# Token halves of the seven products as even and odd tiles, merges from the last group's first half on, gate 1 applied in PSUM

## The chip, the cores and the metric

The kernel runs on one core of a Trainium2 chip. The metric is the device time of one execution in microseconds (us), the median of three runs. Its engines are TensorE (PE, matrix products, with its weight loads as PEld), VectorE (DVE), ScalarE (ACT), GpSimd (POOL) and SyncE (SP), which here issues all DMAs.

## What is computed

One decoder block for 1024 tokens of width 1024: sparse attention and a Mamba-2 mixer side by side, merged by two gates, an output projection, then a SwiGLU network. The part that matters:

```python
x = x + gt1 * ((g_attn * y_attn + g_ssm * y_ssm) @ w_o)
h = rms_norm(x, norm2_w) * (1.0 + sc2) + sh2
x = x + gt2 * ((silu(h @ w_gate) * (h @ w_up)) @ w_down)
return rms_norm(x, norm_f_w)
```

`y_ssm = o_ssm @ w_ssm_out` is summed over four groups of 512 channels; `gt1` (a row of 1024) depends on neither token nor `x`.

## The kernel before

All products keep float32 accuracy with operands split into a high part (a rounded copy, made by ScalarE) and a low part (a difference, made by VectorE or GpSimd), and three matmuls `hi*hi + hi*lo + lo*hi` (`mm3k`, lines 295 to 297). Order is written by hand in a small planner, `Flow`: each engine has a queue, every step says what it needs and an estimated cost, and the steps are emitted in the order in which their engine could take them by these estimates. `first=True` puts a step at the head of its queue. TensorE is fed by generators ("streams") that yield one product at a time; the first stream whose next product is ready goes. On the chip each engine runs its list strictly in that order, waiting on semaphores.

*State-space projection* (`outputs`, `ssm_job`). For group g, token half h (512 tokens) and eight blocks of 128 features ft, one product of 12 matmuls writes PSUM; VectorE adds it into `yacc` (line 1309). The last one, (3, 1), is left to `last_ssm` in the tail.

*Merge* (`merge`, line 1509). For half h and feature block ft: two DMAs bring the gate and the gated attention part, VectorE does two instructions (1519, 1520), ScalarE the high part M0 (1523), VectorE (even ft, 1527) or GpSimd (odd ft, 1525) the low part M1. The merges of half 0 are queued when the tail begins, those of half 1 follow the products of `last_ssm`, one each.

*Out-projection* (`out_proj`). `w_o` comes in column blocks of 256 (`load_wo`, n = 0 to 5, where 4 and 5 are blocks 0 and 1 once more): DMA, GpSimd multiplies with gate 1 (1498), ScalarE and VectorE split (1501, 1502). A product (n, t) takes column block n mod 4 and token tile t (128 tokens) into PSUM [128, 256], three buffers; VectorE adds it to x (1567). `order` lists the 32 products: tiles 0 to 3 with all blocks, then tiles 4 to 7. When a tile has its four blocks, `norm2` stores it, squares it (ScalarE, 1580), takes the root (VectorE, 12 small instructions, lines 259 to 269) and scales it (ScalarE, 1584); `turn_x` turns it round on TensorE (h2T, 1603) and applies scale and shift (1609, 1612).

*Seven products* (`gate_up`). The SwiGLU products are done by Strassen's scheme in the form with seven products: the moving matrix is cut into B11, B21 (first token half; features 0 to 511 and 512 to 1023) and B12, B22 (second half), and combinations T1, T2, T3, T4 of a first-half tile with a second-half tile are made by `add` and `copy` in `turn_x` (1639, 1642) as soon as the second-half tile is turned: five ScalarE steps, of VectorE t1, t2 and two low parts, of GpSimd t3, T3's and T1's low parts and t4; `split_t4` splits T4 at the end. First-half tiles are only split (1625, 1626). The results lie where M0 and M1 had the merged tile, and in E0. `gate_up` begins with the four products that need B11 and B21 alone, then B22, T2 and the others; each waits for all four tiles of its operand. The weight combinations (`ff_pieces`) share VectorE, GpSimd and ScalarE with this.

*Down projection* (`down`). For each token half, 22 steps of eight products; at step 6 of each half one DMA reads that half of x1 back (1932); `final` ends each tile.

Workspace rows of 512 columns come from a ring of 18 (`row`): two in `sl`, which first holds gate 1's row (`gt`) and is given free when wo's last block is multiplied, and sixteen in `ex`.

Of the kernel before, what the change touches and what calls it, by code (L numbers as in the profile page):

```python
# [12 lines left out]
AF = mybir.ActivationFunctionType  # L13
# [226 lines left out]
class Kern:  # L240
# [997 lines left out]
    def outputs(self):  # L1238
# [37 lines left out]
        for g in range(4):  # L1276
            for h in range(2):
                for b in range(2):
                    if (g, h) == (3, 1):
                        self.Wlast = W[3, 0], W[3, 1]  # L1280
                        return
                    w = W[g, b]
                    for m in range(4):
                        op = yield from self.ssm_job(g, h, b, m, w)
                    if h == 1:
                        w.until(op)
                        if g < 3:
                            W[g + 1, b] = self.load_ssm(g + 1, b)
            self.yT[g].until(op)
# [5 lines left out]
    def ssm_job(self, g, h, b, m, w):  # L1295
        nc = self.nc
        A, V, G, D = self.ops()
        while len(self.yTop[g]) < 4 * h + 4:
            yield None
        ft, c, s = 4 * b + m, slice(m * 128, (m + 1) * 128), slice(h * 512, (h + 1) * 512)  # L1300
        ps, yT = self.buf("mm", [128, 512], "sps"), self.yT[g]
        needs = self.yTop[g][4 * h:4 * h + 4]
        for k in range(4):
            op = yield ([w.ops[k], ps] + needs, 0.685, lambda k=k: self.mm3k(
                ps.t, k, 4, w.hi[:, k, c], w.lo[:, k, c], yT[:, 0, k, s], yT[:, 1, k, s]))
        if g == 0:
            x = A(0.48, [op, self.yacc], lambda: nc.scalar.activation(self.yacc[:, ft, s], ps.t, AF.Copy))
        else:
            x = V(0.6, [op], lambda: nc.vector.tensor_tensor(self.yacc[:, ft, s], self.yacc[:, ft, s], ps.t, op=OP.add),
                  first=(g, h) == (3, 1))  # L1310
        ps.until(x)
        self.ssmop = x
        return op
# [100 lines left out]
    def tail(self):  # L1414
# [23 lines left out]
        self.gtop = D(1.46, self.gst[2], lambda: nc.sync.dma_start(self.gt(), self.gtd[0]))  # L1438
        self.wo, self.gtuse = {}, []
        self.kept, self.t4s = [], []  # L1440
        self.norms, self.blk = [], {n: [] for n in ("B11", "B21", "T1", "B22", "T2", "T3", "T4")}
        self.acts = [[None] * 2 for _ in range(NFF)]
        for n in range(2):
            self.load_wo(n)
        for ft in range(8):
            self.merge(0, ft, [])
        for n in range(2, 4):
            self.load_wo(n)
# [35 lines left out]
    def load_wo(self, n):  # L1484

        nc, b = self.nc, n % 4
        A, V, G, D = self.ops()
        if n == 4:
            self.wo[n] = W = Weights(*(Halves(self.buf("x1t", [128, 4, 256], f"x{r}{k}_o{n}", FR) for k in range(2)) for r in range(2)))
        else:  # L1490
            self.wo[n] = W = Weights(*(self.buf(tg, [128, 8, 256], f"{tg}_o{n}", FR) for tg in ("whi", "wlo")))
        room = lambda w, k0: w.bufs[k0 // 4] if n == 4 else w
        cs = slice(256 * b, 256 * b + 256)
        for k0 in (0, 4):
            raw, ks = self.buf("raw", [128, 4, 256], f"wo{n}{k0}"), slice(k0, k0 + 4)
            d = D(1.46, [raw], lambda raw=raw, k0=k0: nc.sync.dma_start(
                raw.t, self.a["w_o"][128 * k0:128 * k0 + 512, cs].rearrange("(k p) c -> p k c", p=128)))
            d = G(2.3, [d, self.gtop], lambda raw=raw: nc.gpsimd.tensor_tensor(
                raw.t, raw.t, self.gt()[:, None, cs].to_broadcast([128, 4, 256]), op=OP.mult))
            self.gtuse.append(d)  # L1500
            x = A(0.95, [d, room(W.hi, k0)], lambda raw=raw, ks=ks: nc.scalar.activation(W.hi[:, ks], raw.t, AF.Copy))
            x = V(1.14, [x, room(W.lo, k0)], lambda raw=raw, ks=ks: nc.vector.tensor_tensor(W.lo[:, ks], raw.t, W.hi[:, ks], op=OP.subtract))
            raw.until(x)
            W.ops += [x] * 4
        if n == 5:
            for i in range(2):
                self.rings["sl"][i] = self.gtuse

    def merge(self, h, ft, needs):
# [11 lines left out]
        u.until(e)  # L1521
        m = lambda t: t[:, 2 * h + ft // 4, ft % 4]
        e = A(0.52, [e, self.M0], lambda: nc.scalar.activation(m(self.M0), y(), AF.Copy))
        if ft % 2:
            e = G(1.23, [e, self.M1], lambda: nc.gpsimd.tensor_tensor(m(self.M1), y(), m(self.M0), op=OP.subtract))
        else:
            e = V(0.6, [e, self.M1], lambda: nc.vector.tensor_tensor(m(self.M1), y(), m(self.M0), op=OP.subtract))
        self.mop[h][ft] = e

    def last_ssm(self):  # L1530

        for ft in range(8):
            op = yield from self.ssm_job(3, 1, ft // 4, ft % 4, self.Wlast[ft // 4])
            if ft % 4 == 3:
                self.Wlast[ft // 4].until(op)
            self.merge(1, ft, [self.ssmop])
        self.yT[3].until(op)
        self.yacc.until(*self.mop[0], *self.mop[1])

    def out_proj(self):  # L1540
# [5 lines left out]
        two = lambda b, t: [(b, t), (b, t + 1), (b + 1, t), (b + 1, t + 1), (b, t + 2), (b + 1, t + 2), (b, t + 3), (b + 1, t + 3)]  # L1546
        order = one(0) + two(2, 0) + [(2, t) for t in fours(4)] + [(n, t) for t in fours(4) for n in (3, 4, 5)]
        left = [4, 4, 8, 8, 4, 4]
        while self.mrg < 16:
            yield None  # L1550
        xop = [D(1.46, [self.x1[t]], lambda t=t: nc.sync.dma_start(self.x1[t].t, a["x"][t * 128:(t + 1) * 128])) for t in range(NT)]
        for n, t in order:
# [5 lines left out]
            for k in range(8):  # L1558
                m = lambda r, k=k: r[:, 2 * (t // 4) + k // 4, k % 4, 128 * (t % 4):128 * (t % 4) + 128]
# [10 lines left out]
            self.x1op[t][b] = e  # L1570
            if None not in self.x1op[t]:
                self.norm2(t, op)

    def norm2(self, t, read):
# [13 lines left out]
    def turn_x(self):  # L1588
# [3 lines left out]
        for _ in range(NT):  # L1592
            while not self.norms:
                yield None
            t, need, read = self.norms.pop(0)
            js = slice(128 * (t % 4), 128 * (t % 4) + 128)
            tfs, es = [], []
# [23 lines left out]
            f4 = lambda h, tfs=tfs: tfs[h].t.rearrange("p (k c) -> p k c", c=128)  # L1621
            if t < 4:
                for h in range(2):
# [3 lines left out]
                    self.blk[("B11", "B21")[h]].append(y)  # L1627
                self.kept.append((tfs, es))
# [294 lines left out]
    def down(self):  # L1923
# [4 lines left out]
        gn = self.buf("h32", [128, 2, 1024], "gn")  # L1928
        x2op = {}

        def load_x2(h):
            x2op[h] = D(4.3, [x2], lambda: nc.sync.dma_start(
                x2[:, 4 * h:4 * h + 4], self.x1d[4 * h:4 * h + 4].rearrange("t p c -> p t c")))

# [5 lines left out]
        for h in range(2):  # L1940
# [7 lines left out]
            for f, t, c in jobs:  # L1948
                if (f, t, c) == (6, 0, 0):
                    load_x2(h)  # L1950
                if (h, f) not in self.dl:
# [18 lines left out]
                e = V(0.6, [e, x2op[h]], lambda y=y, tt=tt, cs=cs: nc.vector.tensor_tensor(  # L1970
                    x2[:, tt, cs], x2[:, tt, cs], y.t, op=OP.add))
# [16 lines left out]
    def final(self, t, nf, nfop):  # L1988
# [362 lines left out]
```

## Time and profile before

| | us |
|---|---|
| median of three runs (2584.51 to 2589.9) | 2586.04 |
| the profiled execution | 2588.99 |
| its span, first to last instruction | 2587.2 |
| TensorE busy | 2480.7 |
| VectorE busy | 1706.9 |
| ScalarE busy | 1221.9 |
| GpSimd busy | 1021.3 |
| mean granted TensorE clock | 0.983 |

Times of the rows count from the span's start. The clock column is the share of full speed that the chip granted. A name like `ops<-whi_o,M` says which tile an instruction writes and which it reads: `sps` a state-space product, `ops` an out-projection product, `h2T` a turned tile, `gu` one of the seven products, `dps` a down product, `ex` and `sl` workspace rows, `x1r`, `whi_pc` and `wlo_pc` pieces of weights.

### The profile page before, as it was taken

The page shows a single profiled execution, that of the slowest core. Times are in us where ns is not written, and L with a number is a line of the kernel's source. Part 1 is how long each engine was busy: PE and PEld are TensorE (multiplying, and loading weights), DVE is VectorE, ACT ScalarE, POOL GpSimd, SP SyncE. Part 2 cuts the span into 40 slices and gives each one's busy share as a digit, 9 for nine tenths or more (in the row PEclk, how much of TensorE's full clock was granted, in tenths as well). Part 3 has the DMA queues.
Part 4 walks back from the last instruction along what each step waited for, and adds up shares of the span by engine and source line. Part 5 has one row for each costly group of instructions (what it writes and reads, how often), then busy time and mean ns, then how long its engine had stood idle before and what let it go on. Part 6 is the DMA issues. An engine that isn't in the chain of part 4 may idle for free. (4 is left out here: it accounts for less than half of the span.)

```text
span 2587.2 us, 39156 instructions
## 1 busy us (share of the span) xinstructions
PE 2480.7 (96%) x13806; PEld 2119.4 (82%) x13806; DVE 1706.9 (66%) x3856; ACT 1221.9 (47%) x2614; POOL 1021.3 (39%) x803
## 2 busy tenths in 40 slices
PE   5999999999999999999998999999989999999997
PEld 5999779799889898888876777788968888888886
DVE  7644887866776678664478686759776545553555
ACT  4421767666556666555556356412543223223332
POOL 2111463636263636264444232115365445442222
PEclk8999999999999999999999999999989999999999
DMA  7433322213133323222456675336222322326362
GB/s 245 133 117 120 107 83 72 77 47 107 45 90 128 105 70 92 60 88 84 127 172 225 214 228 183 106 127 203 91 68 73 95 73 75 98 87 222 119 228 78
DMA packets 226260, 308.02 MB, mean 119 GB/s; under 512 B 17416, under 2 KB 151304, under 8 KB 225552
## 3 DMA queue, kind: packets, MB, share of 16 engines
q1 hardware_dynamic: 226064, 305.52, 37.1%
q8 instruction: 109, 1.79, 0.3%
q14 instruction: 87, 0.71, 0.1%
HBM read 229.83 MB, written 75.63 MB: 118 GB/s over the span
## 5 line engine op out<-in xcount | busy, mean ns | idle before, releaser
L2107 POOL TENSOR_SCALAR P<-P,sm,gate 128x640 f32<-128x640 f32 (+7 forms) x256 | 215.4, 852 | 378.2 <-DVE sm L2104 300.0
L2178 DVE TENSOR_TENSOR kv<-tp,kv 128x512 fp32r<-128x512 f32 (+1 forms) x296 | 189.6, 657 | 118.3 <-ACT kv L2177 116.9
L2177 ACT ACTIVATE kv<-tp 128x512 fp32r<-128x512 f32 (+1 forms) x296 | 165.1, 573 | 193.2 <-PE tp L2174 187.2
L2098 ACT ACTIVATE P<-P,sm 128x640 f32<-128x640 f32 (+7 forms) x256 | 186.8, 732 | 45.2 <-DVE sm L2094 43.8
L1068 PE MATMUL o<-kv 128*128 128x512 f32 x528 | 190.7, 412 | 14.9 <-DVE kv L2178 13.4
L2089 PE MATMUL S<-kv,Q 128*128 128x384 f32 (+5 forms) x768 | 183.0, 336 | 4.2 <-DVE sm L2094 4.2
L2094 DVE CUSTOM_DVE_ANT_0 P<-S,kb 128x256 f32<-128x256 f32 (+5 forms) x256 | 120.5, 495 | 62.7 <-PE tp L2174 33.9
L295 PE MATMUL fps<-hT_hi,whi_x 128*128 128x512 f32 x384 | 157.8, 411 | 0.0
L2174 PE MATMUL tp<-id,P 128*128 128x128 f32 x1056 | 154.9, 274 | 0.0
L1116 DVE SCALAR_TENSOR_TENSOR u<-xr,hcw,u 128x512 f32<-128x512 f32 x144 | 142.2, 988 | 17.6 <-ACT u L1119 12.8
L295 PE MATMUL fps<-whi_z,hT_hi 128*128 128x256 f32 x512 | 151.5, 296 | 0.1
L297 PE MATMUL fps<-hT_hi,wlo_x 128*128 128x512 f32 x384 | 150.9, 393 | 0.0
L296 PE MATMUL fps<-hT_lo,whi_x 128*128 128x512 f32 x384 | 150.6, 392 | 0.0
L2174 PEld LDWEIGHTS tp<-id,P 128*128 128x128 f32 x1056 | 128.7, 141 | 21.5 <-issue 0.4
L2089 PEld LDWEIGHTS S<-kv,Q 128*128 128x128 f32 x768 | 129.4, 190 | 20.6 <-DVE sm L2094 6.2
L297 PE MATMUL fps<-whi_z,hT_lo 128*128 128x256 f32 x512 | 145.8, 285 | 0.0
L296 PE MATMUL fps<-wlo_z,hT_hi 128*128 128x256 f32 x512 | 145.7, 284 | 0.0
L1068 PEld LDWEIGHTS o<-kv 128*128 128x128 f32 x528 | 96.4, 191 | 34.7 <-DVE kv L2178 19.0
L1826 DVE TENSOR_TENSOR ex<-ex,gu 128x512 f32<-128x512 f32 x103 | 69.6, 683 | 74.0 <-PE gu L297 55.4
L295 PE MATMUL gu<-M,x1r 128*128 128x512 f32 x292 | 116.5, 399 | 1.9 <-ACT M L1642 1.9
L296 PE MATMUL gu<-M,x1r 128*128 128x512 f32 x292 | 116.8, 400 | 0.4 <-DVE M L1639 0.4
L297 PE MATMUL gu<-M,x1r 128*128 128x512 f32 x292 | 116.3, 398 | 0.0
(434 smaller groups left out, 7767.9 us busy)
## 6 DMA issues: line engine op xcount, KB each, us to landing
wd<-w_down SPq DMA_DIRECT2D x44, 512.0 KB, 3.4
wada<-w_ada SPq DMA_DIRECT2D x40, 512.0 KB, 4.5
ac<-acd SPq DMA_DIRECT2D x32, 512.0 KB, 4.2
raw_x<-w_in SPq DMA_DIRECT2D x24, 512.0 KB, 4.5
ff<-w_gate SPq DMA_DIRECT2D x22, 512.0 KB
ff<-w_up SPq DMA_DIRECT2D x22, 512.0 KB, 5.3
actd<-ex SPq DMA_DIRECT2D x39, 256.0 KB, 3.1
ex<-actd SPq DMA_DIRECT2D x38, 256.0 KB, 3.7
```

Source lines behind the costliest of these rows:

```text
L295: mm(ps, lh, rh, start=k == 0, stop=False)
L296: mm(ps, lh, rl, start=False, stop=False)
L297: mm(ps, ll, rh, start=False, stop=k == kt - 1)
L1068: nc.tensor.matmul(o.t.rearrange("p h q -> p (h q)"), vst(), pair()[m], start=n + m == 0, stop=n == u.total - 1 and m == 1)
L1116: nc.vector.scalar_tensor_tensor(u.t, xr[:, k:k + N2], hcw[:, ft, k:k + 1], u.t, op0=OP.mult, op1=OP.add)
L2089: mm(sp[:, :w], q, kvb.kv[:, br, r, first + c0:first + c1], start=r == 0, stop=r == 1)
L2094: nc.vector.tensor_tensor_reduce(P[:, c0:c1], sp[:, :w], k.kb[:, m0:m0 + w], scale=-1.0, scalar=sm[:, 0, h:h + 1] if p else 3.0e38, op0=OP ...
L2098: ex = A(0.26 + 0.8333e-3 * n, [mx], lambda: nc.scalar.activation(P[:, :n], P[:, :n], AF.Exp, bias=sm[:, 1, h:h + 1], scale=-1.0, accum_ou ...
L2107: nc.gpsimd.tensor_scalar(P[:, :n], P[:, :n], sm[:, 3, m:m + 1], k.gate[:, i, self.h0 + m, br + 1:br + 2], op0=OP.mult, op1=OP.mult)
L2174: nc.tensor.transpose(tp[:, h * 128:h * 128 + 128], P, k.id)
L2177: hi = A(0.064 + 0.104 * n, [op, pair], lambda: nc.scalar.activation(pair()[0][:, c], tp[:, c], AF.Copy))
L2178: lo = V(0.068 + 0.133 * n, [hi], lambda: nc.vector.tensor_sub(pair()[1][:, c], tp[:, c], pair()[0][:, c]))
```

## The change

Three things. First, the state-space products of (3, 0) are moved into `last_ssm` too, in the same order as before; each is followed by its merge, and `yacc`'s accumulation is put first in VectorE's queue for the whole last group. All four first blocks of `w_o` are queued at the beginning of the tail. Second, the halves of the seven products are the even and the odd tiles: `merge` writes M0 and M1 by parity, `order` takes tiles 4 and 6 before 5 and 7 for the last three blocks, an odd tile t is combined with t-1, and the down projection's halves are even and odd tiles, for which both halves of x1 are read back at step 6 of the first half. Third, `w_o` is no longer multiplied by gate 1; a VectorE instruction multiplies each product in PSUM, before the sum. The second low part of wo block 4 goes to GpSimd. `sl` keeps gate 1 until the last such instruction.

```diff
@@ outputs
-                    if (g, h) == (3, 1):
+                    if (g, h) == (3, 0):
@@ ssm_job
-                  first=(g, h) == (3, 1))
+                  first=g == 3)
@@ tail
-        for n in range(2):
-            self.load_wo(n)
-        for ft in range(8):
-            self.merge(0, ft, [])
-        for n in range(2, 4):
+        for n in range(4):
             self.load_wo(n)
@@ load_wo
-            d = G(2.3, [d, self.gtop], lambda raw=raw: nc.gpsimd.tensor_tensor(
-                raw.t, raw.t, self.gt()[:, None, cs].to_broadcast([128, 4, 256]), op=OP.mult))
-            self.gtuse.append(d)
...
-            x = V(1.14, [x, room(W.lo, k0)], lambda raw=raw, ks=ks: nc.vector.tensor_tensor(W.lo[:, ks], raw.t, W.hi[:, ks], op=OP.subtract))
+            E, eng, cost = (G, nc.gpsimd, 2.3) if n == 4 and k0 else (V, nc.vector, 1.14)
+            x = E(cost, [x, room(W.lo, k0)], lambda raw=raw, ks=ks, eng=eng: eng.tensor_tensor(
+                W.lo[:, ks], raw.t, W.hi[:, ks], op=OP.subtract), first=n > 3)
@@ merge
-        m = lambda t: t[:, 2 * h + ft // 4, ft % 4]
+        m = lambda r: r.t.rearrange("p (t b) k (j c) -> p t b k j c", t=2, c=128)[:, :, ft // 4, ft % 4, 2 * h:2 * h + 2]
+        y4 = lambda: y().rearrange("p (j t c) -> p t j c", t=2, c=128)
...
@@ last_ssm
-        for ft in range(8):
-            op = yield from self.ssm_job(3, 1, ft // 4, ft % 4, self.Wlast[ft // 4])
-            if ft % 4 == 3:
-                self.Wlast[ft // 4].until(op)
-            self.merge(1, ft, [self.ssmop])
+        for h in range(2):
+            for ft in range(8):
+                op = yield from self.ssm_job(3, h, ft // 4, ft % 4, self.Wlast[ft // 4])
+                if h and ft % 4 == 3:
+                    self.Wlast[ft // 4].until(op)
+                self.merge(h, ft, [self.ssmop])
@@ out_proj
-        order = one(0) + two(2, 0) + [(2, t) for t in fours(4)] + [(n, t) for t in fours(4) for n in (3, 4, 5)]
+        order = one(0) + two(2, 0) + [(2, t) for t in fours(4)] + [(n, t) for n in (3, 4, 5) for t in (4, 6)] + [(n, t) for t in (5, 7) for n in (3, 4, 5)]
...
-            e = V(0.34, [op, xop[t]], lambda ps=ps, t=t, cs=cs: nc.vector.tensor_tensor(
+            e = V(0.34, [op, self.gtop], lambda ps=ps, cs=cs: nc.vector.tensor_tensor(
+                ps.t, ps.t, self.gt()[:, cs], op=OP.mult), first=True)
+            e = V(0.34, [e, xop[t]], lambda ps=ps, t=t, cs=cs: nc.vector.tensor_tensor(
                 self.x1[t][:, cs], self.x1[t][:, cs], ps.t, op=OP.add), first=True)
@@ turn_x
-            if t < 4:
+            if t % 2 == 0:
...
-            (r11, r21), old = self.kept[t - 4]
+            (r11, r21), old = self.kept[t - 1]
...
-            old = old + self.blk["B11"] + self.blk["B21"]
+            old = old + self.done2[t - 1]
@@ down
-                if (f, t, c) == (6, 0, 0):
-                    load_x2(h)
+                if (h, f, t, c) == (0, 6, 0, 0):
+                    for u in range(2):
+                        x2op.append(D(4.3, [x2], lambda u=u: nc.sync.dma_start(
+                            x2[:, 4 * u:4 * u + 4], self.x1d[4 * u:4 * u + 4].rearrange("t p c -> p t c"))))
...
-                tt, cs, y = 4 * h + t, slice(512 * c, 512 * c + 512), self.row()
+                tt, cs, y = 2 * t + h, slice(512 * c, 512 * c + 512), self.row()
@@ final
-            if t < 4:
+            if t % 2 == 0:
```

## Rows read from the trace of the kernel before

**Rows 1.** The page, part 1: busy time, share and instructions of TensorE.

```profile
PE 2480.7 (96%) x13806; PEld 2119.4 (82%) x13806; DVE 1706.9 (66%) x3856; ACT 1221.9 (47%) x2614; POOL 1021.3 (39%) x803
```

**Rows 2.** Stretches: length, then PE, PEld, DVE, ACT, POOL busy, clock, DMA share, GB/s.

```profile
1725.00:1747.00 22.00, 22.00 (x99) 18.22 (x98) 8.30 (x13) 2.25 (x4) 4.78 (x2) 1.00 0.56 207
1747.00:1768.00 21.00, 21.00 (x94) 17.38 (x93) 19.93 (x29) 5.69 (x8) 5.60 (x4) 1.00 0.65 200
1768.00:1878.20 110.20, 101.62 (x818) 99.74 (x817) 91.97 (x166) 51.93 (x88) 52.41 (x26) 0.97 0.41 134
1878.20:1918.00 39.80, 28.78 (x104) 21.63 (x104) 34.71 (x48) 19.85 (x37) 27.43 (x19) 0.83 0.23 73
1918.00:2571.00 653.00, 653.00 (x2815) 528.35 (x2814) 337.05 (x447) 203.64 (x361) 261.25 (x192) 1.00 0.34 113
```

**Rows 3.** TensorE's waits, 1768 to 1792: waiting line, releaser, sum, times, longest.

```profile
PE ops L297 <- POOL M L1525: 1.9, 1, 1.9
PE ops L297 <- DVE M L1527: 1.6, 1, 1.6
PE ops L295 <- DVE x L1567: 1.2, 2, 1.0
```

**Rows 4.** TensorE's waits, 1792 to 1878.2.

```profile
PE h2T L1603 <- ACT x L1584: 3.4, 4, 1.4
PE ops L296 <- DVE wlo_o L1502: 0.5, 1, 0.5
```

**Rows 5.** TensorE's waits, 1878.2 to 1918.

```profile
PE h2T L1603 <- ACT x L1584: 3.4, 1, 3.4
PE gu L296 <- DVE E L1639: 2.3, 1, 2.3
PE gu L295 <- ACT M L1642: 1.9, 1, 1.9
PE gu L295 <- ACT whi_pc L1692: 1.5, 1, 1.5
PE gu L297 <- DVE wlo_pc L1694: 1.5, 1, 1.5
PE gu L296 <- DVE M L1639: 0.4, 1, 0.4
```

**Rows 6.** Groups, GpSimd then VectorE, 1718 to 1918: busy, mean ns, idle before, releasers.

```profile
L1498 POOL TENSOR_TENSOR wo<-wo,sl 128x1024 f32<-128x1024 f32 x12 | 32.2, 2701 | 94.2 <-DMA wo<-w_o 79.0 <-DVE wlo_o L1502 11.8 <-DVE x L1567 3.4
...
L1639 POOL TENSOR_TENSOR M<-ex,M 128x512 fp32r<-128x512 f32 x4 | 7.0, 1740 | 0.0
...
L1520 DVE TENSOR_TENSOR yacc<-mg 128x512 f32<-128x512 f32 x16 | 17.2, 1096 | 0.0
...
L1519 DVE SCALAR_TENSOR_TENSOR mg<-mg,yacc 128x512 f32<-128x512 f32 x16 | 13.1, 846 | 0.0
L1309 DVE TENSOR_TENSOR yacc<-yacc,sps 128x512 f32<-128x512 f32 x19 | 13.0, 686 | 20.3 <-PE sps L297 20.1
...
L1527 DVE TENSOR_TENSOR M<-yacc,M 128x512 fp32r<-128x512 f32 x8 | 8.2, 1027 | 0.1
```

**Rows 7.** Timeline of VectorE and ScalarE: start us, duration us, instruction.

```profile
1784.28 2.87 DVE L1520 TENSOR_TENSOR yacc<-mg 128x512 f32<-128x512 f32 x1
1787.07 0.41 DVE L1567 TENSOR_TENSOR x<-x,ops 128x256 f32<-128x256 f32 x1
...
1882.57 0.42 DVE L1567 TENSOR_TENSOR x<-x,ops 128x256 f32<-128x256 f32 x1
...
1894.11 1.15 ACT L1584 ACTIVATE x<-x,rq_n 128x1024 f32<-128x1024 f32 x1 [2.24 <-DVE rq_n L264]
...
1905.54 1.76 DVE L1639 TENSOR_TENSOR E<-ex,E 128x512 fp32r<-128x512 f32 x1
```

**Rows 8.** Line 1567: its instructions, ns min/median/max, first and last start.

```profile
L1567 DVE TENSOR_TENSOR x<-x,ops x32: 406/412/423, 1783.1 to 1882.6; 128x256 f32<-128x256 f32 x32
```

**Rows 9.** Line 1932: its two loads of half of x1 each, issue to landing.

```profile
DMA to landing us min/median/max: 9.4/9.4/9.4
```

More of the change, by code (lines that the diff above doesn't have):

```diff
@@ L1438, in tail @@
         self.gtop = D(1.46, self.gst[2], lambda: nc.sync.dma_start(self.gt(), self.gtd[0]))
-        self.wo, self.gtuse = {}, []
-        self.kept, self.t4s = [], []
+        self.wo = {}
+        self.done2 = {}
+        self.kept, self.t4s = {}, []
         self.norms, self.blk = [], {n: [] for n in ("B11", "B21", "T1", "B22", "T2", "T3", "T4")}
         self.acts = [[None] * 2 for _ in range(NFF)]
-        for n in range(2):
-            self.load_wo(n)
-        for ft in range(8):
-            self.merge(0, ft, [])
-        for n in range(2, 4):
+        for n in range(4):
             self.load_wo(n)
@@ L1497, in load_wo @@
                 raw.t, self.a["w_o"][128 * k0:128 * k0 + 512, cs].rearrange("(k p) c -> p k c", p=128)))
-            d = G(2.3, [d, self.gtop], lambda raw=raw: nc.gpsimd.tensor_tensor(
-                raw.t, raw.t, self.gt()[:, None, cs].to_broadcast([128, 4, 256]), op=OP.mult))
-            self.gtuse.append(d)
             x = A(0.95, [d, room(W.hi, k0)], lambda raw=raw, ks=ks: nc.scalar.activation(W.hi[:, ks], raw.t, AF.Copy))
-            x = V(1.14, [x, room(W.lo, k0)], lambda raw=raw, ks=ks: nc.vector.tensor_tensor(W.lo[:, ks], raw.t, W.hi[:, ks], op=OP.subtract))
+            E, eng, cost = (G, nc.gpsimd, 2.3) if n == 4 and k0 else (V, nc.vector, 1.14)
+            x = E(cost, [x, room(W.lo, k0)], lambda raw=raw, ks=ks, eng=eng: eng.tensor_tensor(
+                W.lo[:, ks], raw.t, W.hi[:, ks], op=OP.subtract), first=n > 3)
             raw.until(x)
             W.ops += [x] * 4
-        if n == 5:
-            for i in range(2):
-                self.rings["sl"][i] = self.gtuse
     def merge(self, h, ft, needs):
@@ L1521, in merge @@
         u.until(e)
-        m = lambda t: t[:, 2 * h + ft // 4, ft % 4]
-        e = A(0.52, [e, self.M0], lambda: nc.scalar.activation(m(self.M0), y(), AF.Copy))
+        m = lambda r: r.t.rearrange("p (t b) k (j c) -> p t b k j c", t=2, c=128)[:, :, ft // 4, ft % 4, 2 * h:2 * h + 2]
+        y4 = lambda: y().rearrange("p (j t c) -> p t j c", t=2, c=128)
+        e = A(0.52, [e, self.M0], lambda: nc.scalar.activation(m(self.M0), y4(), AF.Copy))
         if ft % 2:
-            e = G(1.23, [e, self.M1], lambda: nc.gpsimd.tensor_tensor(m(self.M1), y(), m(self.M0), op=OP.subtract))
+            e = G(1.23, [e, self.M1], lambda: nc.gpsimd.tensor_tensor(m(self.M1), y4(), m(self.M0), op=OP.subtract))
         else:
-            e = V(0.6, [e, self.M1], lambda: nc.vector.tensor_tensor(m(self.M1), y(), m(self.M0), op=OP.subtract))
+            e = V(0.6, [e, self.M1], lambda: nc.vector.tensor_tensor(m(self.M1), y4(), m(self.M0), op=OP.subtract))
         self.mop[h][ft] = e
     def last_ssm(self):
-        for ft in range(8):
-            op = yield from self.ssm_job(3, 1, ft // 4, ft % 4, self.Wlast[ft // 4])
-            if ft % 4 == 3:
-                self.Wlast[ft // 4].until(op)
-            self.merge(1, ft, [self.ssmop])
+        for h in range(2):
[4 more added lines that the diff above has]
+                self.merge(h, ft, [self.ssmop])
         self.yT[3].until(op)
@@ L1546, in out_proj @@
         two = lambda b, t: [(b, t), (b, t + 1), (b + 1, t), (b + 1, t + 1), (b, t + 2), (b + 1, t + 2), (b, t + 3), (b + 1, t + 3)]
-        order = one(0) + two(2, 0) + [(2, t) for t in fours(4)] + [(n, t) for t in fours(4) for n in (3, 4, 5)]
-        left = [4, 4, 8, 8, 4, 4]
+        order = one(0) + two(2, 0) + [(2, t) for t in fours(4)] + [(n, t) for n in (3, 4, 5) for t in (4, 6)] + [(n, t) for t in (5, 7) for n in (3, 4, 5)]
+        left, gtuse = [4, 4, 8, 8, 4, 4], []
         while self.mrg < 16:
@@ L1558, in out_proj @@
             for k in range(8):
-                m = lambda r, k=k: r[:, 2 * (t // 4) + k // 4, k % 4, 128 * (t % 4):128 * (t % 4) + 128]
+                m = lambda r, k=k: r[:, 2 * (t % 2) + k // 4, k % 4, 64 * (t - t % 2):64 * (t - t % 2) + 128]
                 op = yield ([W.ops[k], self.mop[t // 4][k], ps], 0.356, lambda: self.mm3k(
@@ L1570, in out_proj @@
             self.x1op[t][b] = e
+            gtuse.append(e)
             if None not in self.x1op[t]:
                 self.norm2(t, op)
+        for i in range(2):
+            self.rings["sl"][i] = gtuse
     def norm2(self, t, read):
@@ L1595, in turn_x @@
             t, need, read = self.norms.pop(0)
-            js = slice(128 * (t % 4), 128 * (t % 4) + 128)
+            js = slice(64 * (t - t % 2), 64 * (t - t % 2) + 128)
             tfs, es = [], []
@@ L1627, in turn_x @@
                     self.blk[("B11", "B21")[h]].append(y)
-                self.kept.append((tfs, es))
+                    self.done2.setdefault(t, []).append(y)
+                self.kept[t] = tfs, es
                 continue
@@ L1928, in down @@
         gn = self.buf("h32", [128, 2, 1024], "gn")
[L1929 to L1933, printed above, removed]
+        x2op = []
         for h in range(2):
@@ L1969, in down @@
                 ps.until(e)
-                e = V(0.6, [e, x2op[h]], lambda y=y, tt=tt, cs=cs: nc.vector.tensor_tensor(
+                e = V(0.6, [e, x2op[tt // 4]], lambda y=y, tt=tt, cs=cs: nc.vector.tensor_tensor(
                     x2[:, tt, cs], x2[:, tt, cs], y.t, op=OP.add))
```

## The prediction

> **What bounds the kernel now.** I read the page first. TensorE is busy for 2480.7 us, 96% of the span [rows 1], so a change gains only where TensorE idles or runs at the lower clock. The stretches by stage come next [rows 2]. While the state-space products of the last group run (1725 to 1768), TensorE is full at clock 1.00. From 1918 to 2571 (all but the first of the seven products, and the down projection) it is full again, with no wait. Between them lie the out-projection (1768 to 1878.2, 101.62 of 110.20 us busy, clock 0.97) and the turn into the seven products (1878.2 to 1918, 28.78 of 39.80 us, clock 0.83). All that this change can give back is there.
>
> The idle time, from TensorE's waits: start of the out-projection 1.9 + 1.6 + 1.2 = 4.7 us [rows 3], rest of it 3.4 + 0.5 = 3.9 us [rows 4], the turn 3.4 + 2.3 + 1.9 + 1.5 + 1.5 + 0.4 = 11.0 us [rows 5]. Together 19.6 us, which is what the stretches leave: (110.20 - 101.62) + (39.80 - 28.78) [rows 2]. The two clock levels are 1.2 and 2.4 GHz, so a mean of 0.97 over 110.2 us costs 0.03 x 110.2 = 3.3 us of work and 0.83 over 39.8 us costs 6.8 us; part of the slow time fell on idle time, so I take 3.1 and 6.0. The clock fell behind the idle stretches only, as the full stages at 1.00 show. Loss of this region: start 7.8, middle 3.9, turn 17.0, sum 28.7 us. A change that hides everything here ends 28.7 us earlier.
>
> Who is late? VectorE. It is busy 19.93 of 21 us while the first merges run and 91.97 of 110.20 us in the out-projection, but 8.30 of 22 us in the 22 us before [rows 2]: merging starts with group 3's second half, so eight merges queue beside eight more, beside wo's low parts. GpSimd makes it worse: a 128x512 sum takes VectorE 686 ns in the mean where one operand lies in PSUM [rows 6], while one of two SBUF operands took 2.87 us beside GpSimd's gate multiplication [rows 7], and the sixteen of that kind 1096 ns in the mean [rows 6].
>
> **Part by part.**
>
> **Merges begin with (3, 0).** The eight products of (3, 0) are the same work at the same place (TensorE is full either way). What moves is the merging of half 0: eight merges of two instructions of about 0.69 us, four low parts on VectorE and four on GpSimd, from 1747 on into 1725 to 1750. The instruction after a 2.87 us one starts 0.08 us before that one's end [rows 7], so by starts a merge costs 1.2 us, a low part and an accumulation 0.6 each. The 22 us of eight products [rows 2] are 5.5 us per two, in which VectorE gets 2 x 0.6 + 2 x 1.2 + 0.6 = 4.2 us: 77%, plus what GpSimd's low part blocks. With the means of the merges as they ran beside the gate (0.846, 1.096, 1.027) [rows 6] it is 2 x 0.686 + 2 x 1.942 + 1.027 = 6.28 us, and TensorE would be held back 0.8 us per pair, 6.3 us over eight pairs. Those means come from beside GpSimd's 128x1024 instructions, which go; the remaining block is one 128x512 instruction per pair. I take 1 us (0 to 6.3). The merges' sixteen DMA pairs are spread from two bursts to one pair per 2.7 us behind the wo loads on SP; eight buffers let them run ahead, so nothing. At 1768 half 0 lies merged since some 16 us and half 1 is 2 to 5 us from it, used only 16 products later, so the first two waits of [rows 3] and the clock's fall behind them go; x's loads find their buffers earlier too. Start after: 1 us in place of 7.8.
>
> **Gate 1 in PSUM.** Removed: twelve GpSimd instructions, 32.2 us, mean 2701 ns [rows 6], each a step of 2.4 us or more between wo's load and its split, and each a block for VectorE. Added: 32 VectorE multiplications of 128x256 in PSUM. No row shows an instruction that reads and writes PSUM. The nearest is the sum that follows it, 406 to 423 ns in all 32 [rows 8], never stretched by GpSimd; by starts 0.08 us less, 0.33. I take that: 32 x 0.33 = 10.6 us of VectorE, less than the blocks that go (the merges' 16 sums, 16 products and 8 low parts ran at 1096, 846 and 1027 instead of 686 ns: 6.6 + 2.6 + 2.7 = 11.9 us). From below, nothing is gained by it; from above, 1.76 us as for a contended 128x512 [rows 7]. In the chain of a tile it adds one step of 0.4 us. The 0.5 us wait for wo's low part [rows 4] goes, since wo 5's chain loses 2.4 us and is first used two products later.
>
> The Trainium skill, "SBUF — State Buffer", section "Who interferes with whom", says that a VectorE instruction with two SBUF inputs and a GpSimd instruction that reads SBUF exclude each other for a whole instruction, and that one with at most one SBUF input doesn't take part. The trace agrees on both (2.87 us against 406 to 423 ns). By it the new multiplication is free of GpSimd, and the price 10.6 us stands; but the combinations that move ahead (next part) would bring GpSimd's blocks into the middle.
>
> **wo 4's second low part** goes from VectorE to GpSimd (at most the 2.7 us of a gate instruction of the same shape [rows 6]); its column block is first used at product 23, so free.
>
> **Even and odd halves.** A combination of tiles needs a pair (t-1, t), until now (t-4, t). Four VectorE, four GpSimd and five ScalarE instructions per pair: two of the four sets move from the end into the middle, where tiles 1 and 3 are ready after products 12 and 16 of 32; tiles 4 and 6 need only the simple split. In the turn about 2 x 7 us of GpSimd (1.74 us each [rows 6]) and 2 x 3 to 2 x 7 us of VectorE disappear. What stays is the last tile's own chain, and here I am careful. Before: the last product ends near 1878.4, its sum starts at 1882.57 behind queued work, the normalised tile leaves ScalarE at 1894.11 + 1.15 = 1895.3, its T2 low part ends at 1905.54 + 1.76 = 1907.3 [rows 7]: 29 us. Four products of 2.7 us that need only the even half (10.9 us) cover part of it, as before. After: no 4.2 us delay of the sum (1 us with the gate), the square root and the scaling 6 to 10 us instead of 12.7 since tile 5's set still runs through it, combinations 6 to 9 us: 13 to 20 us against 11 of cover, then the third products. That leaves 2 to 9 us idle, and half as much of the clock again. TensorE's order is fixed from estimates, so part of the waits for the normalised tile stays. Turn after: 8.5 us (3 to 17).
>
> Middle after: the waits for the normalised tiles (3.4 us [rows 4]) lose the gate's blocks and gain those of the combinations. I take 3.5 us (2 to 7).
>
> **Rest.** Two rows of workspace come free only at the end of the out-projection: 16 of 18 remain, and fewer tiles are held at once: nothing. x1 is read back in two loads in a row (9.4 us each to landing [rows 9]) in place of one per half; the stage has no TensorE wait with one such load in each half, and weights are loaded three steps ahead: nothing (0 to 9.4). The final steps are the same in number and order.
>
> **Sum.** After: 1 + 3.5 + 8.5 = 13.0 us of loss for 28.7 before: 15.7 us less. The profiled execution took 2588.99 us, 1.8 us around its span of 2587.2; so 2571.5 of span, 2573.3 in all. The median of the three runs is 2586.04, 2.95 below the profiled one; the same difference gives 2570.3, and I say 2570.
>
> **Rivals.**
> *All hidden.* If VectorE, freed from GpSimd, brings the last tile in 13 us, the loss is 0 + 2 + 3 = 5: 2562. For: VectorE's blocks were the cause in [rows 6]. Against: the square root still queues behind combinations.
> *The turn stays.* If the last tile's chain is as long as before (all its steps remain, the pair before it still ends 8.5 us ahead), only the start and 0.4 of the middle go: 7.2 us, 2579.
> *VectorE holds the merging stage.* TensorE full at 1725 to 1768 becomes its waiting place, 6.3 instead of 1 us: 2576.
> *Slower: the gate's multiplication is dear.* VectorE's demand in the out-projection is 92 us now; about 22 us of merges and their blocks and 12 of other blocks go, 10 of combinations come: 68 us + 32 p for the 98 us that TensorE needs. From p = 0.94 us it bounds; at p = 1.76 us the stage grows by 26 us: 2596. Against: the same PSUM operand at 406 to 423 ns.
> *It does not do what it says* is excluded: the four products that open the turn use only the even half, whose last tile is ready six products earlier.
>
> **How the numbers follow.** Forecast (10 to 21 us less) 0.47; all hidden 0.16; turn stays 0.20; merging stage 0.07; neither gain nor loss 0.04; slower 0.06. The range takes the bounds 5 us (2562) and the turn that stays with a larger middle: 2561 to 2582. 0.2% is 5.2 us, about what a measurement of this kernel can tell from no change: faster 0.47 + 0.16 + 0.15 + 0.07 = 0.85 (a quarter of the turn that stays falls within 0.2%), same 0.05 + 0.04 = 0.09, slower 0.06.
>
> **What would show it.** Right: no TensorE wait for M at the start of the out-projection and clock 1.00 there; TensorE full through the sixteen last state-space products; sums and gate at about 0.41 us; out-projection over 9 to 10 us earlier; idle of the turn under 7 us. Wrong: accumulations late with TensorE idle in the state-space products, a gate multiplication near 0.9 us, or waits for the normalised tile or T2 as long as before.

## The result, and the profile after

The changed kernel took 2564.33 us in the median of 4 runs (2557.07 to 2567.39), the kernel before 2587.97 us beside it: ratio 0.9904, 95% interval 0.9877 to 0.993. Measured again (`a_again`, below): 2566.4 us against 2585.36, ratio 0.992 (0.9904 to 0.9937), so 19 to 24 us less. The forecast was 2570 us, and its sum 15.7 us less than before.

The profiled execution took 2557.07 us, 31.9 us less than that of before. Not all of it is the change. When the k-th matmul of one trace is set beside the k-th of the other, 13.4 us of the distance are there at the first state-space product (`sps`, of group 0), ahead of everything that the change touches. The largest steps (4.3, 2.6, 1.5, 4.8 us) lie where the clock fell in the trace of before, in code that is the same; others, of up to 1.6 us, go both ways. The stretches from 60 us to that product, before and after (columns as in [rows 2]):

```profile
60.00:1541.60 1481.60, 1438.46 (x8798) 1257.79 (x8796) 1028.87 (x2693) 823.32 (x1888) 621.96 (x525) 0.99 0.36 111
60.00:1528.20 1468.20, 1431.59 (x8794) 1251.36 (x8793) 1027.97 (x2693) 822.43 (x1887) 623.70 (x525) 1.00 0.36 112
```

TensorE's work took 6.9 us longer there before, and its idle time was 6.5 us longer. In the other traces that product starts anywhere from 1532.2 to 1546.2 us, without order. I therefore compare stages, from the first matmul of one kind to the first of the next:

| stage, us | before | after | difference |
|---|---|---|---|
| all state-space products, first `sps` to first `ops` | 226.6 | 226.5 | -0.1 |
| out-projection, first `ops` to first `gu` | 110.1 | 97.9 | -12.2 |
| seven products, first `gu` to first `dps` | 447.9 | 441.8 | -6.1 |
| down projection | 245.8 | 245.7 | -0.1 |

That is 18.3 to 18.5 us less for what was changed, close to the 19.0 of the repeat. First the stretches of after, which answer to [rows 2] (length, then PE, PEld, DVE, ACT, POOL busy, clock, DMA share, GB/s):

```profile
1711.50:1733.50 22.00, 22.00 (x99) 18.22 (x98) 19.27 (x29) 5.97 (x10) 4.45 (x3) 1.00 0.83 288
1733.50:1754.50 21.00, 21.00 (x95) 17.38 (x94) 20.12 (x28) 6.32 (x9) 5.22 (x3) 1.00 0.41 135
1754.50:1852.60 98.10, 97.13 (x819) 96.68 (x818) 76.13 (x180) 48.77 (x82) 26.76 (x17) 1.00 0.43 149
1852.60:1892.40 39.80, 32.46 (x131) 24.28 (x130) 31.90 (x52) 20.93 (x37) 26.57 (x18) 0.91 0.24 73
1892.40:2539.00 646.60, 646.60 (x2788) 523.23 (x2787) 337.45 (x444) 201.74 (x358) 257.92 (x189) 1.00 0.34 114
```

VectorE now merges through both first stretches (19.27 us of 22 where it had 8.30, then 20.12 of 21), and TensorE stays full. In the out-projection TensorE works 97.13 of 98.10 us, and VectorE falls from 91.97 to 76.13 us, GpSimd from 52.41 to 26.76. The turn keeps a hole: TensorE is busy 32.46 of 39.80 us, at clock 0.91.

TensorE's waits (line, releaser, sum, times, longest). There is none from 1700 to 1778, where [rows 3] had 4.7 us. From 1778 to 1852.6, for [rows 4]:

```profile
PE h2T L1603 <- ACT x L1584: 1.0, 2, 0.5
```

and from 1852.6 to 1900, for [rows 5]:

```profile
PE gu L295 <- ACT x1r L1693: 2.9, 1, 2.9
PE gu L296 <- DVE E L1640: 2.0, 1, 2.0
PE h2T L1603 <- DVE ex L1612: 1.1, 1, 1.1
PE gu L296 <- DVE M L1640: 0.5, 1, 0.5
PE gu L295 <- DVE ex L1612: 0.5, 1, 0.5
PE h2T L1603 <- ACT ex L1609: 0.3, 1, 0.3
```

From 1900 to 2560 none again. The new instruction and the sum behind it (line 1564, was 1567), ns min/median/max, as in [rows 8]:

```profile
L1562 DVE TENSOR_TENSOR ops<-ops,sl x32: 417/432/433, 1759.8 to 1854.2; 128x256 f32<-128x256 f32 x32
...
L1564 DVE TENSOR_TENSOR x<-x,ops x32: 403/420/422, 1760.7 to 1855.2; 128x256 f32<-128x256 f32 x32
```

Groups of VectorE over 1704 to 1892.4 that answer to [rows 6] (1512 and 1513 are the merge's two instructions, 1521 its low part; busy, mean ns, idle before):

```profile
L1512 DVE SCALAR_TENSOR_TENSOR mg<-mg,yacc 128x512 f32<-128x512 f32 x16 | 13.2, 828 | 1.8 <-DMA mg<-mgd 1.6
...
L1513 DVE TENSOR_TENSOR yacc<-mg 128x512 f32<-128x512 f32 x16 | 12.5, 787 | 0.2
...
L1521 DVE TENSOR_TENSOR M<-yacc,M 128x512 fp32r<-128x512 f32 x8 | 6.0, 747 | 0.1
```

The merge's sums fell from 1096 to 787 ns and its low parts from 1027 to 747; the products hardly (846 to 828).

The timeline of the last tile and of the wait that is new, for [rows 7] (start, duration, instruction; in brackets the idle time before it and its releaser). The last `ops` matmul ends at 1852.8; the first row is the tile's last sum, the second the low part of its T2, the third a combination of weights:

```profile
1855.20 0.41 DVE L1564 TENSOR_TENSOR x<-x,ops 128x256 f32<-128x256 f32 x1
...
1872.47 1.75 DVE L1640 TENSOR_TENSOR E<-ex,E 128x512 fp32r<-128x512 f32 x1
...
1877.54 1.75 DVE L1712 TENSOR_TENSOR ex<-ff,ex 128x512 f32<-128x512 f32 x1
```
```profile
1858.95 1.15 ACT L1584 ACTIVATE x<-x,rq_n 128x1024 f32<-128x1024 f32 x1
...
1879.32 0.63 ACT L1693 ACTIVATE x1r<-ex 128x512 fp32r<-128x512 f32 x1 [2.74 <-DVE ex L1712]
```
```profile
1880.00 0.79 PE L295 MATMUL gu<-M,x1r 128*128 128x512 f32 x1 [2.90 <-ACT x1r L1693]
```

The tile's chain, from the last matmul to the end of that low part, is 1874.2 - 1852.8 = 21.4 us (29 before). The longest single wait left belongs to no token tile: VectorE makes a combination of *weights* (1712) at 1877.54, ScalarE splits it (1693), and the third product with the second weight matrix can start only then.

### The profile page after: what moved, and what is told of

It is laid out like the page before. It is cut to its first block, busy times and chain, and to the rows that moved or that the text cites. A ratio compares the mean times of both kernels' runs of the same rounds, so it can differ in the third digit from the quotient of the medians.

```text
span 2555.3 us, 39172 instructions
## 1 busy us (share of the span) xinstructions
PE 2467.0 (97%) x13806; PEld 2108.4 (83%) x13806; DVE 1698.1 (66%) x3887; ACT 1221.9 (48%) x2614; POOL 992.9 (39%) x792
## 5 line engine op out<-in xcount | busy, mean ns | idle before, releaser
L1827 DVE TENSOR_TENSOR ex<-ex,gu 128x512 f32<-128x512 f32 x117 | 79.0, 684 | 121.6 <-PE gu L297 110.0
L1068 PEld LDWEIGHTS o<-kv 128*128 128x128 f32 x528 | 95.4, 189 | 32.5 <-DVE kv L2177 16.8
L295 PE MATMUL gu<-M,x1r 128*128 128x512 f32 x296 | 117.5, 397 | 2.9 <-ACT x1r L1693 2.9
L1695 POOL TENSOR_TENSOR x1r<-wd,x1r 128x512 fp32r<-128x512 f32 x41 | 54.8, 1337 | 168.1 <-ACT x1r L1693 161.4
L296 PE MATMUL gu<-M,x1r 128*128 128x512 f32 x296 | 117.9, 398 | 0.5 <-DVE M L1640 0.5
```

Of the source, the lines that this page charges most:

```text
L295: mm(ps, lh, rh, start=k == 0, stop=False)
L296: mm(ps, lh, rl, start=False, stop=False)
L1068: nc.tensor.matmul(o.t.rearrange("p h q -> p (h q)"), vst(), pair()[m], start=n + m == 0, stop=n == u.total - 1 and m == 1)
```

## The experiments

The theory: the start was lost to merges that came too late, the middle to GpSimd's gate instructions, the turn to combinations made after the last tiles, so the three parts give their gains one by one. The rival: VectorE's in-order queue is the one cause, and the parts replace each other or depend on each other. The stages of these kernels, in us (one profiled execution of each; the rows `e1` to `e4` ran on one chip, where the kernel before took 2588.95):

| kernel | time | out-projection | seven products |
|---|---|---|---|
| before | 2588.99 | 110.1 | 447.9 |
| `e1_merges` | 2581.43 | 101.8 | 449.2 |
| `e2_gate` | 2577.24 | 102.2 | 448.5 |
| `e3_halves` | 2586.1 | 113.4 | 439.7 |
| `e4_merges_gate` | 2569.93 | 97.9 | 450.4 |
| `e10_gate_halves` | 2573.47 | 102.5 | 441.1 |
| after | 2557.07 | 97.9 | 441.8 |

**The merges alone.** The kernel before, with

```diff
-                    if (g, h) == (3, 1):
+                    if (g, h) == (3, 0):
...
+        for h in range(2):
+            for ft in range(8):
...
+                self.merge(h, ft, [self.ssmop])
```

and, as in the change, `yacc`'s accumulation first in VectorE's queue and all four blocks of `w_o` queued at the beginning of the tail.

> Kernel before with the first part alone: the products of (3, 0) and the merges that follow them in last_ssm. Measures: out-projection stage, from the first out-projection matmul to the first of the seven products (before 110.1 us, changed kernel 97.9), and seven-product stage, from there to the first down-projection matmul (447.9 and 441.8). Theory (the start was late because sixteen merges queued on VectorE in one place): out-projection 102 to 104, no wait for M at its start. Rival (it was late because GpSimd's gate multiplications block VectorE): 108 or more, the waits for M stay. Seven-product stage within 1.5 us of 447.9 by both.

The out-projection became 8.3 us shorter (101.8 us, just under the theory's 102 to 104). The stretch, columns as above, and TensorE's waits in it, 1767.2 to 1869:

```profile
1767.20:1869.00 101.80, 97.95 (x818) 96.69 (x817) 77.95 (x152) 48.50 (x82) 44.41 (x24) 1.00 0.41 144
```
```profile
PE h2T L1600 <- ACT x L1581: 3.3, 3, 1.4
PE ops L296 <- DVE wlo_o L1498: 0.4, 1, 0.4
PE ops L295 <- DVE x L1564: 0.2, 1, 0.2
```

The loss at the start is gone and the clock is 1.00, while the middle stands as in [rows 4]. In the last sixteen state-space products TensorE waits 0.6 us, once, for an accumulation into `yacc`, although GpSimd's gate instructions still ran beside the merges. The whole state-space stage took 229.7 us, 3.1 more than before; the changed kernel has it at 226.5 and 228.5 in two profiles, so I don't lay that on the merges.

**The gate alone.** The kernel before, without GpSimd's multiplication in `load_wo`, with the low parts of `w_o`'s blocks 4 and 5 placed as in the change, and with

```diff
+            e = V(0.34, [op, self.gtop], lambda ps=ps, cs=cs: nc.vector.tensor_tensor(
+                ps.t, ps.t, self.gt()[:, cs], op=OP.mult), first=True)
```

> Kernel before with the third part alone: gate 1 applied in PSUM by VectorE, wo without GpSimd's multiplication. Measures as in e1_merges. Theory (merges queue in one place): VectorE still has sixteen merges around the start, out-projection 104 to 107. Rival (GpSimd's blocks): 99 to 101, waits for M gone. Seven-product stage within 2 us of 447.9 by both.

It gave 7.9 us in the out-projection: 102.2 us, which is neither the theory's 104 to 107 nor the rival's 99 to 101. Waits there, 1764.6 to 1866.8:

```profile
PE ops L295 <- DVE x L1565: 2.5, 1, 2.5
PE ops L296 <- DVE wlo_o L1500: 0.6, 1, 0.6
```

The waits for the normalised tiles are gone, and so are both waits for M at the start: merges that are as late as before, but not blocked, come almost in time. Left at the start is a wait of 2.5 us for x, and the clock is 0.98. So the waits for M have two cures, either of which is enough. 8.3 and 7.9 don't add up to 16.2; with both it is 12.2 (`e4`).

**The halves alone.** The kernel before with the parity layout, the order of products and the two loads of x1 together.

```diff
-        order = one(0) + two(2, 0) + [(2, t) for t in fours(4)] + [(n, t) for t in fours(4) for n in (3, 4, 5)]
+        order = one(0) + two(2, 0) + [(2, t) for t in fours(4)] + [(n, t) for n in (3, 4, 5) for t in (4, 6)] + [(n, t) for t in (5, 7) for n in (3, 4, 5)]
...
-            (r11, r21), old = self.kept[t - 4]
+            (r11, r21), old = self.kept[t - 1]
```

> Kernel before with the second part alone: even and odd tiles as halves, the new order of products, both loads of x1 in the first half of the down projection; merges and gate as before. Theory (the combinations of tiles 1 and 3 moved out of the turn shorten it): seven-product stage 441 to 443. Rival (the turn is shorter because VectorE comes to it without a backlog from merges and gate): 446 or more. Out-projection 108 to 112 by both. The down projection has no TensorE wait by both.

The stretch of the out-projection and its wait for normalised tiles:

```profile
1769.50:1882.90 113.40, 102.30 (x817) 100.89 (x816) 91.47 (x168) 53.19 (x89) 55.05 (x29) 0.95 0.39 131
```
```profile
PE h2T L1605 <- ACT x L1586: 5.4, 3, 2.8
```

The turn gave 8.2 us and the out-projection took 3.3 back: the waits for normalised tiles grew from 3.4 to 5.4 us, with GpSimd at 55.05 us and clock 0.95. Beside the gate in PSUM the halves cost the out-projection 0.3 us (`e10`, below, against `e2`) or nothing (after against `e4`). So what the halves move into the middle is paid there as long as the gate runs on GpSimd.

**Merges and gate, without the halves.** `e1` and `e2` together.

> First and third part together, halves as before. Theory: out-projection 97 to 100, seven-product stage 446 to 449, so that the even and odd tiles alone give the 6 us of the turn. Rival (the turn follows VectorE's backlog): seven-product stage 443 or less.

The out-projection is that of after, 97.9 us at clock 1.00. All of the loss in the turn stays and grows by 2.5 us (450.4 us, over the theory's 446 to 449). Its waits for weights, 1857.9 to 1899, and the longest of them:

```profile
PE gu L297 <- DVE x1r L1692: 8.6, 2, 5.0
PE gu L295 <- ACT x1r L1690: 2.9, 1, 2.9
```
```profile
1866.29 0.80 PE L297 MATMUL gu<-M,x1r 128*128 128x512 f32 x1 [4.98 <-DVE x1r L1692]
```

`x1r` are pieces of weights. The wait of 2.9 us that surprised in the turn of after was already there, for the same product. The longest, 5.0 us, comes in the second of the fourteen products: the low part that it needs stands in VectorE's queue behind combinations of tile 6, which in after needs only its simple split; there this wait is gone. In all, waits for weights are 11.5 us here against 3.0 in [rows 5], and those for token tiles 2.3 against 8.0: 2.8 us more in sum, which is about what the turn grew by.

**Gate and halves, merges late.** `e2` and `e3` together.

> Gate in PSUM and even/odd halves, merges as in the kernel before. Theory (the start is on time only with both, the early merges and GpSimd without the gate): out-projection 101 to 103 as with the gate alone (102.2), seven-product stage 441 to 443 as in the changed kernel. Rival (the early merges are needless beside the other two): 99 or less.

The out-projection's waits:

```profile
PE ops L295 <- DVE x L1567: 2.8, 1, 2.8
PE h2T L1606 <- ACT x L1587: 1.0, 2, 0.5
```

Seven products 441.1, as after; out-projection 102.5 with the wait of 2.8 us for x at its start and clock 0.98. The early merges are needed for the last 4.6 us. In the out-projection the rival holds: the parts replace each other and depend on each other. In the turn the gain is the halves'. That the three single gains add up nearly to the whole in the out-projection (8.3 + 7.9 - 3.3 = 12.9 against 12.2) is chance: 12.2 comes from two of them. Merges and halves without the gate were not run.

**Is the gate's multiplication hidden?** After, with the multiplication made twice (gate 1 squared):

```diff
+            e = V(0.34, [e, self.gtop], lambda ps=ps, cs=cs: nc.vector.tensor_tensor(
+                ps.t, ps.t, self.gt()[:, cs], op=OP.mult), first=True)
```

> Changed kernel with the gate's VectorE multiplication in PSUM done twice (32 more instructions of 128x256; gate 1 enters squared). Measures: out-projection stage (97.9 us in the changed kernel, 97.9 with merges and gate alone) and seven-product stage (441.8). Theory (0.42 us by duration and 0.33 by starts, VectorE has 22 of 98 us free): out-projection 98 to 99, seven-product stage up to 1 longer, since the last tile's chain has one more step of 0.4 us. Rival (VectorE bounds the out-projection, the price of a multiplication shows in full): 106 or more.

And after without it (gate 1 left out):

```diff
-            e = V(0.34, [op, self.gtop], lambda ps=ps, cs=cs: nc.vector.tensor_tensor(
-                ps.t, ps.t, self.gt()[:, cs], op=OP.mult), first=True)
-            e = V(0.34, [e, xop[t]], lambda ps=ps, t=t, cs=cs: nc.vector.tensor_tensor(
+            e = V(0.34, [op, xop[t]], lambda ps=ps, t=t, cs=cs: nc.vector.tensor_tensor(
```

> Changed kernel without the gate's multiplication at all (gate 1 is left out of the computation), which prices the 32 instructions by their absence. Theory (the first 32 are hidden, the second 32 of e5_gate_twice were not): out-projection 97 to 98 against 97.9, seven-product stage 440 to 442 against 441.7. Rival (they cost as much as the second 32, 4.7 and 2.3 us): 93 to 95 and 439 or less; for the out-projection this can be but little, as TensorE idles 1 us there.

| | none (`e9`) | once (after) | twice (`e5`) |
|---|---|---|---|
| out-projection | 98.1 | 97.9 | 102.6 |
| VectorE busy in it | 67.85 | 76.13 | 83.10 |
| seven products | 441.2 | 441.8 | 444.0 |
| time | 2572.11 | 2557.07 | 2577.53 |

The out-projection of `e5`, and TensorE's waits in it:

```profile
1768.00:1870.60 102.60, 98.18 (x817) 97.78 (x816) 83.10 (x207) 47.94 (x82) 26.25 (x17) 0.98 0.41 143
```
```profile
PE h2T L1605 <- ACT x L1586: 2.4, 1, 2.4
PE ops L296 <- DVE x_o L1497: 2.0, 1, 2.0
```

The first 32 cost at most 0.6 us in these two stages. VectorE's busy time grows by 8.28 / 32 = 0.26 us for each; that is a net figure, since in `e9` other VectorE instructions ran longer (the splits of line 1626, 1624 there, 1013 ns in the mean against 680). (`e9`'s whole time is the longer one: its first `sps` came at 1543.9, by the chance above.) The second 32 cost 7 us, between the theory and the rival, though VectorE still had 19 us free by its busy time: TensorE waits 2.4 us for a normalised tile and 2.0 us for a low part of `w_o`, at clock 0.98. Free time in the sum was no cover here. The planner also emits another order when steps are added or left out (the longest wait in `e9`'s turn is 5.0 us for a low part of a token tile), and this and the longer chain of a tile were not told apart.

**Are GpSimd's blocks what keeps the turn long?** After, with the token combinations of GpSimd on VectorE:

```diff
-            t3 = add(G, [t1, es[1]], b12, b22, b12)
+            t3 = add(V, [t1, es[1]], b12, b22, b12)
...
-            t3l = add(G, [t3h], T3l, b12, T3h)
-            t4 = add(G, [t2], b21, b21, u2)
-            t1l = add(G, [t1h, t2], T1l, b11, T1h)
+            t3l = add(V, [t3h], T3l, b12, T3h)
+            t4 = add(V, [t2], b21, b21, u2)
+            t1l = add(V, [t1h, t2], T1l, b11, T1h)
```

> Changed kernel with the four GpSimd steps of each tile pair's combinations (t3, low parts of T1 and T3, t4) on VectorE. Theory (a GpSimd step of 1.7 us blocks VectorE for about 1.1 us, its own VectorE time is 0.6 us, so the rest of the turn's loss is GpSimd's blocks): seven-product stage 436 to 440 against 441.8. Rival (VectorE's queue is the bound and sixteen more instructions, 9.6 us, lengthen it): 443 or more. Out-projection 97 to 99 by both.

and, beyond that, T4's low parts and the first block's weight combinations on VectorE too:

> As e6_comb_dve, and the split of T4 and the GpSimd steps of the first two weight blocks on VectorE too, so that GpSimd does next to nothing from the out-projection to the thirteenth of the seven-product stage's products. Theory (blocks): 434 to 439 in the seven-product stage, VectorE's 128x512 instructions there at 0.69 us and none near 1.75. Rival (VectorE is the bound): 444 or more.

The same group of combinations in the turn, first after, then `e7_turn_dve` (busy, mean ns, idle before), and the turn of `e7_turn_dve`:

```profile
L1640 DVE TENSOR_TENSOR ex<-ex 128x512 f32<-128x512 f32 x4 | 5.1, 1291 | 0.0
```
```profile
L1640 DVE TENSOR_TENSOR ex<-ex 128x512 f32<-128x512 f32 x8 | 5.3, 686 | 0.0
```
```profile
1870.50:1912.00 41.50, 32.42 (x132) 25.23 (x131) 32.99 (x68) 21.67 (x39) 8.53 (x6) 0.88 0.23 70
```

With GpSimd at 8.53 us in place of 26.57 the blocks are gone from this group: 686 ns each, twice the work in the same time. The Trainium skill, "SBUF — State Buffer", section "Who interferes with whom", says that a VectorE instruction with two SBUF inputs contends with a GpSimd instruction that reads SBUF; the trace agrees, with 1291 and 686 ns. Yet the seven products took 442.2 (`e6`) and 443.0 (`e7`) against 441.8, not the 434 to 440 of the theory. So to move this work to VectorE gains nothing; what the blocks alone cost it doesn't tell, since VectorE has more to do (68 instructions in the turn against 52). The out-projection, which I had not expected to change, took 105.1 and 103.8 against 97.9, with waits of 3.9 and 2.9 us for a low part of `w_o`: its last one started 79 and 78 us after the stage's first matmul, and 70 us in after. What was left to test is the order in VectorE's queue.

**The same kernel again.** No edit, to see how far its time and stages vary.

> The changed kernel once more, timed in five rounds. Theory (18 us come from the out-projection and the turn; the 13 us by which its first profile was ahead at the first state-space product are chance, as that product starts between 1528 and 1542 us in six profiles of unchanged code ahead of it): ratio 0.992 to 0.994, 16 to 20 us; first state-space product again anywhere in 1528 to 1542. Rival (the changed order also shortens what lies ahead): 0.990 or less, and the first state-space product at 1528 to 1530.

2566.4 us in the median of 6 (2562.63 to 2569.8); stages 97.9 and 441.7 us. So in two profiles of this kernel these two stages repeat within 0.1 us while the whole varies by 7; the state-space stage doesn't (228.5 against 226.5). In its merging stretch TensorE waits 0.4 us once for `yacc`.

**Another order of the seven products.** If the weight combinations for the second matrix are late, products that don't need them should go first. After, with

```diff
-        seq = [(0, 0, 1), (1, 0, 1), (0, 0, 2), (1, 0, 2), (0, 0, 3), (0, 0, 6), (1, 0, 3), (0, 0, 7), (1, 0, 6), (0, 0, 5), (1, 0, 7),
+        seq = [(0, 0, 1), (1, 0, 1), (0, 0, 2), (1, 0, 2), (0, 0, 3), (0, 0, 6), (0, 0, 7), (0, 0, 5), (1, 0, 3), (1, 0, 6), (1, 0, 7),
```

(first the weight matrix, then the block, then the product).

> Changed kernel with another order of the first fourteen of the seven-product stage's products: after B22 and T2 of the first weights come their T3 and T1 and only then the second weights' B22. Theory (what is left of the turn is VectorE's queue; the second weights' combinations are the last to come through it, and the product that waits 2 to 3 us for them stands ahead of two that need none of them): the wait of gu for ACT x1r falls under 1 us, seven-product stage 437.5 to 440 against 441.7, total 2 to 4 us under the changed kernel's 2566. Rival (T3's and T1's low parts on GpSimd are as late, so the wait only changes its name): 441 or more.

The turn, 1871.2 to 1911.2, columns as above, and its TensorE waits:

```profile
1871.20:1911.20 40.00, 36.83 (x157) 28.86 (x157) 37.88 (x57) 23.23 (x41) 29.00 (x19) 0.96 0.24 73
```
```profile
PE gu L296 <- DVE E L1640: 1.2, 1, 1.2
PE h2T L1603 <- DVE ex L1612: 1.1, 1, 1.1
PE gu L295 <- DVE ex L1612: 0.5, 1, 0.5
PE h2T L1603 <- ACT ex L1609: 0.3, 1, 0.3
```

The 2.9 us wait is gone, and the seven products took 435.6 us, 6.1 to 6.2 less than after. In the turn TensorE idles 3.2 us in place of 7.3, and the clock is 0.96 in place of 0.91, which is another 2 us of 40. The kernel took 2561.5 us (4 runs, 2558.52 to 2568.32) against 2585.92 of the kernel before: ratio 0.990 (0.9881 to 0.9919). By its stages it is the best of all here; its median is 3 to 5 us under those of after, but those were taken on other chips, and the intervals of the ratios overlap, so the whole time alone doesn't tell the two kernels apart.

## Why the prediction was right

**What bounds the kernel: right.** All of the gain that the stages show lies where TensorE idled or ran slowly; the stages that were full before take the same time.

**The total: right, in part by luck: its terms were off on both sides.**

| loss, us | before | forecast | after |
|---|---|---|---|
| start | 7.8 | 1 | 0 |
| middle | 3.9 | 3.5 | 1.0 |
| turn | 17.0 | 8.5 | 7.3 idle + 0.09 x 39.8 = 3.6 clock = 10.9 |
| sum | 28.7 | 13.0 | 11.9 |

28.7 - 11.9 = 16.8 us; the stages became 18.3 us shorter. The rest is the clock term of before: the same out-projection kept TensorE busy 101.62 us before and 97.13 after, so slower matmuls cost 4.5 us there, not the 3.1 that I had taken. The start and the middle gave 3.5 us more than forecast and the turn 2.4 less. My sum gave the out-projection 7.2 us and my sign for it said 9 to 10, which don't agree; it measured 12.2.

**Merges: right in effect, incomplete in cause.** Full TensorE at VectorE 19.27 of 22 and 20.12 of 21 us rules out the rival of the merging stage at 6.3 us; against the price of 1 us the waits for `yacc` there are 0 (after), 0.4 (`a_again`) and 0.6 us (`e1`). But `e2` shows that the start's waits for M come from the blocks as much as from the late merges: the gate alone removes them, the merges alone as well. By my parts the gate would have given little; alone it gave 7.9.

**Gate in PSUM: right.** 417 to 433 ns beside 403 to 422 for the sum, and VectorE's demand came to 76.13 us against my 68 + 32 x 0.33 = 78.6. That it was hidden because some 20 us of VectorE were free was not reason enough: with twice as many, 19 us were still free and the stage took 4.7 us longer. Of the rival "slower" nothing showed.

**The middle: priced too high.** I feared that combinations would bring GpSimd's blocks there, at 3.5 us. `e3` shows that this happens (5.4 us of waits), but only beside the gate instructions; without them 1.0 us is left.

**The turn: mis-sized by 2.4 us, and the wait misnamed.** The mechanism held (`e3`: -8.2 us alone). Its idle time of 7.3 us (6.4 in `a_again`) stands at the 7 that I had named as a sign. The last tile took 21.4 us, just over my 13 to 20: its sum came 2.4 us after the product instead of 1, root and scaling from the sum at 1855.20 to 1860.1 were 4.9 instead of 6 to 10, the combinations 14.1 instead of 6 to 9, since they still run among GpSimd's steps and weight combinations. The step that failed is that I followed only this tile's chain. The longest wait, 2.9 us at 1880.0, is for weights that queue behind it on VectorE; `e4` has it too, and `e8`, where it is gone, gives 6.1 us. Had I read which `DVE` items stand in the queue behind T2 [rows 7], and that [rows 5] already held 3.0 us of waits for pieces of weights, it could have been in the sum.

**Free edits: right.** The down projection is 245.7 us against 245.8 with no wait, and over all profiles it takes 244.5 to 245.8 us with one load in each half and 244.1 to 246.0 with two in a row, so the two loads in a row [rows 9] cost nothing that shows; nor do the fewer rows of the ring show as a wait.

**Open:** how much of `e5` is order and how much the longer chain; what GpSimd's blocks alone cost the turn; and whether it is the turn's earlier start that lets `e1` and `e4` lengthen the seven products by 1.3 and 2.5 us. Their waits say only where: for normalised tiles in `e1` (5.8 us against 3.4), for weights in `e4`.

## What to carry to other kernels

Price an idle stretch by every item that the late engine still has queued, not by one chain: when the first late item comes in time, the next in the queue is the new wait, and an order that asks for it later (here 6 us of a stage for one line) can be worth more than work moved to another engine. Two edits that cure the same wait don't add, so measure each alone and both together. On a kernel whose whole time varies by 7 us or more, compare the stages in question from first matmul to first matmul: the two that mattered here repeated within 0.1 us in two profiles.

## What was not expected of the hardware

An instruction of VectorE that reads and writes PSUM (417 to 433 ns, 128x256 float32) costs hardly more than one that reads PSUM and writes SBUF (403 to 422 ns). Moving GpSimd's combinations to VectorE took the blocks off a group of its instructions (1291 to 686 ns each), and the stage became no shorter (443.0 us against 441.8). And TensorE's clock fell at places in unchanged code in one execution and not in the next: from 505 to 515 us of the trace of before it was 0.66, and in the same code of after, 504 to 511 us, 1.00. Slower work (6.9 us) and more idle time (6.5 us) in that code made 13.4 us between two profiles.
